# Attention products: another order of PSUM banks, row copies on GpSimd, casts behind bank copies, joint exponentials

## The chip, the cores and the metric

The kernel runs on one core of one Trainium2 chip. It is written in Python with a tile framework that places tiles, inserts semaphores and orders the instructions of each engine. The metric is the device time of one execution in microseconds (us); the median of several runs is compared. A profile of one execution shows each instruction's start and length on five engines: TensorE (PE; its weight loads are PEld), VectorE (DVE), ScalarE (ACT), GpSimd (POOL) and SyncE (SP, which here only issues DMAs).

## The reference: what is computed

One sequence of 512 tokens of width 1024 passes two layers, each a mixer and a SwiGLU feed-forward block. The change touches only the mixer of the first layer, dilated window attention:

```python
proj = (xn @ w_in).reshape(B, S, N_GROUPS, 3, ATTN_HEADS, ATTN_HEAD_DIM)
for g, (window, dilation) in enumerate(((128, 1), (512, 4), (2048, 16))):
    q = apply_partial_rope(proj[:, :, g, 0], positions) * scale
    k = apply_partial_rope(proj[:, :, g, 1], positions)
    o, lse = dilated_window_attention(q, k, proj[:, :, g, 2], window, dilation)
wts = jax.nn.softmax(jnp.stack(lses), axis=0)
o = jnp.einsum('gbsh,gbshd->bshd', wts, jnp.stack(outs))
```

There are 8 heads of 128 and three groups of queries, keys and values. Group 0 attends to a window of 128 neighbours; groups 1 and 2 see every 4th and every 16th token. Only the first 32 of a head's 128 dimensions are rotated by position (`apply_partial_rope`). The three groups' results are joined by a softmax over their log sums. After attention come the output projection and the feed-forward block; the second layer has an mLSTM mixer and another feed-forward block. All matrices are fp32.

## The kernel before

**Products in three parts.** A fp32 matrix is split into a high part, rounded to a shorter format (a cast on ScalarE, L223), and a low part, the rest (a subtraction on VectorE, L225). A product is the sum of high x high, high x low and low x high (`SPLITS`).

**Head pairs.** Heads are worked on in four pairs (`pr` 0 to 3). For each pair `project_pair` makes queries and keys of the three groups. Group 0 is a plain product (`project`, two chunks of weights for q and two for k, 128x512 matmuls). Groups 1 and 2 of pairs 1 to 3 go through `qk_unit`: a Strassen-like scheme of seven half-size products with 24 matmuls of 128x256 each, in the order P1, P5, P6, P2, P7, P3, P4. Their sums live in three PSUM banks: `c11` (P1, P2), `p5` (P5, P3) and `u` (P6, P7, P4). `u` starts as a copy of P1's result, made by ScalarE (L905), and P6 adds to it. After each product `finish` empties or combines a bank: P5 and P6 are copied to `vu` (L908, L910), P2 and P4 go to the query tile by two ScalarE copies (L899 takes the 32 rows to be rotated, L918 all 128), and P7 and P3 are added to `vu` on VectorE (L925). The tag `acc` has three banks in all; who asks for a bank gets one that has come free and waits for its last reader.

**Weights.** `feed` holds a plan of weight preparations. `prepare_part` subtracts weight blocks on VectorE where a product needs it (L873), splits the block (L223, L225) and issues the next loads on SP (L865). `feed.pop` takes the next prepared weights, `feed.fill(n)` prepares until `n` are ready, three to four products ahead.

**Rotation.** `rope` rotates the packed 32 rows on VectorE (L607 to L616) and returns `back`, which copies the rotated rows back into the query and key tiles. For the plain products (`blocks` true) these are eight copies of 32x256 on ScalarE (L622); they are put off by three ticks in pairs 1 to 3.

**Attention of the pair before.** While pair `pr` is projected, attention of pair `pr - 1` runs between its products. A counter of ticks orders this: `advance` adds one and runs what is due. Group 0 of a pair has four ticks; in `qk_unit` a tick falls after P5, P2, P3 and P4. `RUN_AT` gives the ticks, counted from the pair's start: scores of groups 1 and 2 at 1 (`scores12`), the five steps of `rest` at 4, 5, 8, 8, 9, values at 11 and 12, loads of values at 2, 3, 1. Scores of group 0 (`scores0`) of the pair now projected come at its tick 10.

Scores are masked on VectorE (L706, L727), which also takes row maxima; `exponentials` runs on ScalarE: for group 0 four per head (L743), for groups 1 and 2 eight per head (L749) of 128x128, whose sums are added on VectorE (L751). `joint` computes the weights of the groups, `weigh` multiplies them in (L794, L797), `transposes` turns the probabilities in blocks of 32 (L803) and writes them to DRAM by four DMAs (L806), `bring` reads them back transposed (L811), and `values` multiplies them with the values (L821, L826) into a bank of tag `o`, which `scores0` uses too.

**What sets the order.** The framework puts instructions on each engine's queue in the order in which the kernel traces them, unless an earlier one is not ready by its own plan; then a later one may go ahead. Explicit edges restrict this: `issue_after(ins)` puts what is traced inside it behind `ins` on the same engine. `behind_scores` puts weight subtractions behind the last masking of group 0's scores (`ahead_of_splits`), `behind_factors` puts weight casts behind the ScalarE instruction kept in `ahead_of_casts`, and `behind(fn, engine=ACT)` puts a function's ScalarE work behind the last that was traced. Each engine then runs its queue strictly in order. DMAs of the attention steps are issued by POOL, loads of weights by SP.

Of the kernel before, what the change touches and what calls it, by code (L numbers as in the profile page):

```python
# [36 lines left out]
RUN_AT = (1, (4, 5, 8, 8, 9), (11, 12), (2, 3, 1))  # L37
# [36 lines left out]
def tile_hybrid_dilated_attn_mlstm(  # L74
# [329 lines left out]
    with ExitStack() as actx:  # L404
# [198 lines left out]
        def rope(qk, rot, blocks, first=0, end=4, direct=False):  # L603

            at = slice(R * first, R * end)
            a, sh = rot[0][at], rot[1][at]
            nc.vector.stream_shuffle(sh, a, shift)  # L607
            nc.vector.tensor_tensor(a, a, cosn[at], op=ALU.mult)
            nc.vector.tensor_tensor(sh, sh, sinn[at], op=ALU.mult)
            two_m = lambda t: t.rearrange("p (m s) -> p m s", m=2)  # L610
            if direct:
                for q in range(first, end):
                    nc.vector.tensor_tensor(halves(qk[q // 2][:R], q % 2), two_m(rot[0][quarter(q)]),
                                            two_m(rot[1][quarter(q)]), op=ALU.add)
                return
            nc.vector.tensor_tensor(a, a, sh, op=ALU.add)  # L616

            def back():
                for q in range(first, end):
                    if blocks:  # L620
                        for m in range(2):
                            nc.scalar.activation(turned(qk, q, m, True), packed(rot, q, m, True), AF.Copy)  # L622
                    else:
                        nc.scalar.activation(halves(qk[q // 2][:R], q % 2), two_m(rot[0][quarter(q)]), AF.Copy)
            return back
# [28 lines left out]
        def attention_pair(pr, qks):  # L654
# [3 lines left out]
            dn = ap2.tile([P, 2, 2, 4], F32, tag="dn", name=nm + "dn", bufs=2)  # L658
# [32 lines left out]
            def scores0(q, k):  # L691
# [19 lines left out]
                for i in range(2):  # L711
                    exponentials(0, i)
# [21 lines left out]
            def exponentials(o, i):  # L734
# [11 lines left out]
                for g in (1, 2):  # L746
                    for c in range(4):
                        blk = p12[i][:, 4 * (g - 1) + c, :]
                        nc.scalar.activation(blk, blk, AF.Exp, bias=nb[:, 1, i, c:c + 1], scale=QK_SCALE,  # L749
                                             accum_out=dn[:, g - 1, i, c:c + 1])  # L750
                nc.vector.tensor_tensor(own[:, 1, 1, i], dn[:, 0, i], dn[:, 1, i], op=ALU.add)  # L751
# [85 lines left out]
            rest = (first_rest, lambda: transposes(0), lambda: weigh(1), lambda: (transposes(1), bring(0)),  # L837
# [52 lines left out]
        def qk_unit(pr, g, qk):  # L890
# [10 lines left out]
            def finish(name):  # L901
                nonlocal rot, vu
                if name == "P1":
                    acc["u"] = acc_tile(nm + "u")
                    nc.scalar.activation(acc["u"], acc["c11"], AF.Copy)  # L905
                elif name == "P5":
                    vu = ap.tile([P, 2, SEQ], F32, tag="vu", name=nm + "vu")
                    nc.scalar.activation(vu[:, 0], acc["p5"], AF.Copy)  # L908
                elif name == "P6":
                    nc.scalar.activation(vu[:, 1], acc["u"], AF.Copy)  # L910
                elif name in ("P2", "P4"):
# [6 lines left out]
                    nc.scalar.activation(halves(qk[0], th), src, AF.Copy)  # L918
                    if last and th:
                        rope(qk, rot, False, 1, 2, True)  # L920
                else:
# [9 lines left out]
            for n, name in enumerate(QK_ORDER):  # L931
                key = target[name]
                if name in ("P1", "P5"):
                    acc[key] = acc_tile(nm + key)
                whl = feed.pop()
# [12 lines left out]
                feed.fill(feed.ahead + 1)  # L948
# [6 lines left out]
                if n in (1, 3, 5, 6):  # L955
                    advance()

        def project_pair(pr, qks, then=None):
            nm = "a%d" % pr
            for g in range(3):  # L960
# [18 lines left out]
                for part in range(2):  # L979
# [24 lines left out]
                    if part == 1:  # L1004
# [3 lines left out]
                        else:  # L1008
                            back = turn()
                            defer(3 if pr else 1, lambda back=back: behind(back, engine=ACT))  # L1010
# [1360 lines left out]
```

## Time and profile before

| what | us |
|---|---|
| median of 3 runs | 1405.29 |
| lowest and highest of them | 1402.56, 1406.05 |
| profiled execution, its own time | 1400.59 |
| its span, first to last instruction | 1398.8 |

The profile names a group of instructions by line, engine, operation, the tile written and the tiles read, and its shape. "Busy" is time in which the engine works; a wait is idle time before an instruction, put down to what released it. In a timeline row the numbers are the start and the length; in square brackets stand the idle time before it and its releaser. A row of windows gives for a stretch its length, then for each engine the busy time and the number of instructions, then the share of full speed that TensorE's clock was granted, the busy share of the DMA engines and GB/s. In names, `a1g2p` is bank `p5` of pair 1, group 2, `P_h` and `P_l` are the high and low parts of product weights, `W` a weight block, `a0pB` and `a0pT` the turned and the fetched probabilities of pair 0, `a1s` scores and `a1o` values of pair 1. Tile names drop numbers, so `P_h` stands for every product.

### The profile page before, as it was taken

To read this page: it belongs to the slowest core of one execution; us is meant where nothing else is said; L and a number is where in the kernel's file an instruction comes from. 1 tells how busy PE (TensorE), PEld (TensorE's weight loads), DVE (VectorE), ACT (ScalarE), POOL (GpSimd) and SP (SyncE) were. 2 spreads that over 40 slices of the span, in tenths; PEclk is the share of its full clock that TensorE was granted. 3 is DMA by queue.
4 is the path that set the end of the run, shared out by engine and by line. 5 is a ranking of instruction groups with operands and counts; after the bars stand their busy time and mean duration, and the time that the engine had idled before them with its cause. 6 is when DMAs were issued, how large, how long until landed. Compare 5 with 4: busy or idle time off the path is not lost. (4 is left out here: it accounts for less than half of the span.)

```text
span 1398.8 us, 22646 instructions
## 1 busy us (share of the span) xinstructions
PE 1374.3 (98%) x8740; PEld 1247.2 (89%) x8740; DVE 1110.6 (79%) x1853; ACT 799.1 (57%) x1334; POOL 163.8 (12%) x240
## 2 busy tenths in 40 slices
PE   9999999999999999999999999999999999999997
PEld 7888889989988888999999998898888899999886
DVE  7758768595878289877877898898858987888887
ACT  5556565756665155445566464786534544458854
POOL 3000011111001001000000100113201240001213
PEclk9999999999999999999999999999999999999999
DMA  8534246538274447333253643324334563335963
GB/s 288 181 120 136 83 144 194 161 95 258 76 266 141 159 130 158 121 121 115 91 164 84 159 129 93 91 76 106 99 113 117 139 189 121 121 107 132 199 164 101
DMA packets 140068, 193.82 MB, mean 139 GB/s; under 512 B 8980, under 2 KB 104788, under 8 KB 139960
## 3 DMA queue, kind: packets, MB, share of 16 engines
q1 hardware_dynamic: 119552, 139.81, 31.3%
q0 software_dynamic: 18752, 51.43, 15.6%
q8 instruction: 69, 1.13, 0.3%
q10 hardware_dynamic: 1656, 1.12, 0.2%
q14 instruction: 39, 0.32, 0.1%
HBM read 167.30 MB, written 22.54 MB: 136 GB/s over the span
## 5 line engine op out<-in xcount | busy, mean ns | idle before, releaser
L1674 POOL DMA_DIRECT2D f1T<-in_ffn_w_out_dram x15 | 17.8, 1186 | 209.1 <-DMA f1P_2w_w<-in_ffn_w_out_dram 136.6
L1649 POOL DMA_DIRECT2D f0S<-in_ffn_w_out_dram x10 | 8.8, 886 | 259.6 <-DVE f0hid L1566 173.1
L2206 POOL DMA_DIRECT2D hD<-hB x32 | 21.8, 698 | 68.5 <-DVE hB L2203 68.5
L255 PE MATMUL mo<-n_h,mo_k_l 128*128 128x512 f32 x64 | 25.3, 395 | 0.0
L255 PE MATMUL mo<-n_h,mo_k_h 128*128 128x512 f32 x64 | 25.2, 394 | 0.0
L255 PE MATMUL mo<-n_l,mo_k_h 128*128 128x512 f32 x64 | 25.2, 393 | 0.0
L255 PE MATMUL awo<-ao_h,awo_k_h 128*128 128x512 f32 x64 | 25.2, 393 | 0.0
L255 PE MATMUL mqk<-n_h,mqk_k_h 128*128 128x512 f32 x64 | 25.1, 392 | 0.0
L255 PE MATMUL mwo<-yo_l,mwo_k_h 128*128 128x512 f32 x64 | 25.1, 392 | 0.0
L255 PE MATMUL mqk<-n_l,mqk_k_h 128*128 128x512 f32 x64 | 25.1, 392 | 0.0
L255 PE MATMUL awo<-ao_l,awo_k_h 128*128 128x512 f32 x64 | 25.0, 391 | 0.0
L255 PE MATMUL f0j<-n_h,f0j_h 128*128 128x512 f32 x64 | 25.0, 391 | 0.0
L255 PE MATMUL f1j<-n_h,f1j_h 128*128 128x512 f32 x64 | 25.0, 391 | 0.0
L255 PE MATMUL mwo<-yo_h,mwo_k_l 128*128 128x512 f32 x64 | 25.0, 391 | 0.0
L255 PE MATMUL mqk<-n_h,mqk_k_l 128*128 128x512 f32 x64 | 25.0, 390 | 0.0
L255 PE MATMUL awo<-ao_h,awo_k_l 128*128 128x512 f32 x64 | 25.0, 390 | 0.0
L255 PE MATMUL f0j<-n_h,f0j_l 128*128 128x512 f32 x64 | 24.9, 390 | 0.0
L255 PE MATMUL f1j<-n_h,f1j_l 128*128 128x512 f32 x64 | 24.9, 390 | 0.0
L255 PE MATMUL f0j<-n_l,f0j_h 128*128 128x512 f32 x64 | 24.9, 389 | 0.0
L255 PE MATMUL f1j<-n_l,f1j_h 128*128 128x512 f32 x64 | 24.9, 389 | 0.0
L255 PE MATMUL mwo<-yo_h,mwo_k_h 128*128 128x512 f32 x64 | 24.8, 391 | 0.0
L225 DVE TENSOR_TENSOR v1P_l<-v1W,v1P_h 128x1024 fp32r<-128x1024 f32 x14 | 17.1, 1224 | 9.3 <-ACT v1P_h L223 9.3
(2617 smaller groups left out, 5899.7 us busy)
## 6 DMA issues: line engine op xcount, KB each, us to landing
f0j_w<-in_ffn_w_in_dram SPq DMA_DIRECT2D x17, 512.0 KB, 5.2
f1j_w<-in_ffn_w_in_dram SPq DMA_DIRECT2D x17, 512.0 KB, 6.1
f1T<-in_ffn_w_out_dram POOLq DMA_DIRECT2D x15, 512.0 KB, 7.0
f0hid<-in_ffn_w_in_dram SPq DMA_DIRECT2D x9, 512.0 KB, 5.7
f1hid<-in_ffn_w_in_dram SPq DMA_DIRECT2D x9, 512.0 KB, 4.9
v0W<-in_attn_w_in_dram SPq DMA_DIRECT2D x8, 512.0 KB, 6.4
v1W<-in_attn_w_in_dram SPq DMA_DIRECT2D x8, 512.0 KB, 3.7
awo_k_w<-in_attn_w_out_dram SPq DMA_DIRECT2D x8, 512.0 KB, 6.3
```

Of the source, the lines that this page charges most:

```text
L225: nc.vector.tensor_tensor(lo[:, :n], raw[:, :n], hi[:, :n].bitcast(F32), op=ALU.subtract)
L255: nc.tensor.matmul(acc, whl[a][:, k, m * P:(m + 1) * P], pairs[b][kk], start=(kk == 0 and (a, b) == SPLITS[0]), stop=(kk == nk - 1 and (a, ...
L1649: nc.gpsimd.dma_start(t, src[1][:, ks], accum_op=ALU.add)
L1674: nc.gpsimd.dma_start(view(to), weight_rows(hk * UNITS + u, n), accum_op=ALU.add)
L2206: nc.gpsimd.dma_start(hD[k // 4].rearrange("(b i) x -> i b x", i=R)[:, :, c0:c0 + R], t[R * a_:R * (a_ + 1)])
```

## The change

Seven edits, all in the attention mixer:

1. In `qk_unit`, bank `u` is asked for, and filled from `c11`, ahead of P5's matmuls and after P5's own bank, no longer right after P1.
2. The copies of rotated rows of the plain products (pairs 1 to 3) move from ScalarE, three ticks late, to GpSimd, one tick late.
3. After each bank copy `ahead_of_casts` is set to it, so later weight casts stand behind it on ScalarE.
4. `feed.fill` comes after `advance` instead of ahead of it, not after P1, and once more ahead of P5.
5. Exponentials of groups 1 and 2 share one instruction of 128x256 per block; the tile `dn` and the additions at L751 go.
6. In the last pair, group 0's exponentials are put off by two ticks and stand behind ScalarE's other work.
7. The first head's transposed probabilities are fetched (`bring(0)`) at tick 7 as a step of its own; it was done at tick 8 after the second transpose.

```diff
--- before.py
+++ after.py
@@ -34,7 +34,7 @@
 C2 = float(np.float32(np.uint32(np.float32(TWO_PI - C1).view(np.uint32) & 0xFFFFF000).view(np.float32)))
 C3 = float(np.float32(TWO_PI - C1 - C2))
 SCORES0_AT = 6
-RUN_AT = (1, (4, 5, 8, 8, 9), (11, 12), (2, 3, 1))
+RUN_AT = (1, (4, 5, 7, 8, 8, 9), (11, 12), (2, 3, 1))
 LAST_AT = (1, (2,), (), (1, 1, 1))
 STACK_AT = (9, 11, 15, 17)
 HEAD_AT = ((9, 10, 12), (10, 11, 13), (12, 13, 15), (13, 14, 16), (15, 16, 18), (16, 17, 19), (18, 19, 21),
@@ -615,11 +615,15 @@
                 return
             nc.vector.tensor_tensor(a, a, sh, op=ALU.add)
 
-            def back():
+            def back(by_pool=False):
                 for q in range(first, end):
                     if blocks:
                         for m in range(2):
-                            nc.scalar.activation(turned(qk, q, m, True), packed(rot, q, m, True), AF.Copy)
+                            to, src = turned(qk, q, m, True), packed(rot, q, m, True)
+                            if by_pool:
+                                nc.gpsimd.tensor_copy(to, src)
+                            else:
+                                nc.scalar.activation(to, src, AF.Copy)
                     else:
                         nc.scalar.activation(halves(qk[q // 2][:R], q % 2), two_m(rot[0][quarter(q)]), AF.Copy)
             return back
@@ -655,7 +659,6 @@
             nm = "a%d" % pr
             mx = ap2.tile([P, 2, 2, 4], F32, tag="mx", name=nm + "mx", bufs=2)
             nb = ap2.tile([P, 2, 2, 4], F32, tag="nb", name=nm + "nb", bufs=2)
-            dn = ap2.tile([P, 2, 2, 4], F32, tag="dn", name=nm + "dn", bufs=2)
             own = ap2.tile([P, 2, 2, 2, 4], F32, tag="own", name=nm + "own", bufs=2)
             oth = ap2.tile([P, 2, 2, 2, 4], F32, tag="oth", name=nm + "oth", bufs=2)
             p, p0, p12 = [], [], []
@@ -708,8 +711,14 @@
                                 sp[:, o:o + w], mask_band[:, 2 * P - w:], 1.0, -3e38,
                                 op0=ALU.add, op1=ALU.max, accum_out=own[:, 0, 0, i, b:b + 1])
                 ahead_of_splits[0] = last_on(DVE)
-                for i in range(2):
-                    exponentials(0, i)
+
+                def exps():
+                    for i in range(2):
+                        exponentials(0, i)
+                if pr < HEADS // 2 - 1:
+                    exps()
+                else:
+                    defer(2, lambda: behind(exps, engine=ACT))
 
             banks_ = {}
 
@@ -743,12 +752,10 @@
                         nc.scalar.activation(blk, blk, AF.Exp, bias=nb[:, 0, i, b:b + 1], scale=QK_SCALE,
                                              accum_out=own[:, 1, 0, i, b:b + 1])
                     return
-                for g in (1, 2):
-                    for c in range(4):
-                        blk = p12[i][:, 4 * (g - 1) + c, :]
-                        nc.scalar.activation(blk, blk, AF.Exp, bias=nb[:, 1, i, c:c + 1], scale=QK_SCALE,
-                                             accum_out=dn[:, g - 1, i, c:c + 1])
-                nc.vector.tensor_tensor(own[:, 1, 1, i], dn[:, 0, i], dn[:, 1, i], op=ALU.add)
+                for c in range(4):
+                    blk = p12[i].rearrange("p (g c) k -> p c g k", g=2)[:, c]
+                    nc.scalar.activation(blk, blk, AF.Exp, bias=nb[:, 1, i, c:c + 1], scale=QK_SCALE,
+                                         accum_out=own[:, 1, 1, i, c:c + 1])
 
             def exchange():
 
@@ -834,7 +841,7 @@
             def first_rest():
                 joint()
                 weigh(0)
-            rest = (first_rest, lambda: transposes(0), lambda: weigh(1), lambda: (transposes(1), bring(0)),
+            rest = (first_rest, lambda: transposes(0), lambda: bring(0), lambda: weigh(1), lambda: transposes(1),
                     lambda: bring(1))
             if pr == HEADS // 2 - 1:
                 def all_rest():
@@ -900,14 +907,13 @@
 
             def finish(name):
                 nonlocal rot, vu
-                if name == "P1":
-                    acc["u"] = acc_tile(nm + "u")
-                    nc.scalar.activation(acc["u"], acc["c11"], AF.Copy)
-                elif name == "P5":
+                if name == "P5":
                     vu = ap.tile([P, 2, SEQ], F32, tag="vu", name=nm + "vu")
                     nc.scalar.activation(vu[:, 0], acc["p5"], AF.Copy)
+                    ahead_of_casts[0] = last_on(ACT)
                 elif name == "P6":
                     nc.scalar.activation(vu[:, 1], acc["u"], AF.Copy)
+                    ahead_of_casts[0] = last_on(ACT)
                 elif name in ("P2", "P4"):
                     th = int(name == "P4")
                     src = two_m(acc[target[name]])
@@ -916,9 +922,10 @@
                         rot = t[:, 0], t[:, 1]
                     pack(th, src[:R])
                     nc.scalar.activation(halves(qk[0], th), src, AF.Copy)
+                    ahead_of_casts[0] = last_on(ACT)
                     if last and th:
                         rope(qk, rot, False, 1, 2, True)
-                else:
+                elif name in ("P7", "P3"):
                     th = int(name == "P7")
                     out = halves(qk[1], th)
                     with behind_scores():
@@ -932,6 +939,11 @@
                 key = target[name]
                 if name in ("P1", "P5"):
                     acc[key] = acc_tile(nm + key)
+                if name == "P5":
+                    acc["u"] = acc_tile(nm + "u")
+                    nc.scalar.activation(acc["u"], acc["c11"], AF.Copy)
+                    ahead_of_casts[0] = last_on(ACT)
+                    feed.fill(feed.ahead + 1)
                 whl = feed.pop()
                 with fenced():
                     for m in range(2):
@@ -945,7 +957,6 @@
                                                  start=(name in ("P1", "P5") and m == 0 and k == 0 and (a, b) == SPLITS[0]),
                                                  stop=(m == 1 and k == 3 and (a, b) == SPLITS[-1]), skip_group_check=True)
                 finish(name)
-                feed.fill(feed.ahead + 1)
                 if n == 6 and not last:
                     back = rope(qk, rot, False)
                     if g == 2:
@@ -954,6 +965,8 @@
                         defer(1, lambda: behind(back, engine=ACT))
                 if n in (1, 3, 5, 6):
                     advance()
+                if n:
+                    feed.fill(feed.ahead + 1)
 
         def project_pair(pr, qks, then=None):
             nm = "a%d" % pr
@@ -1007,7 +1020,7 @@
                             postponed.append(lambda: turn()())
                         else:
                             back = turn()
-                            defer(3 if pr else 1, lambda back=back: behind(back, engine=ACT))
+                            defer(1, (lambda back=back: back(True)) if pr else lambda back=back: behind(back, engine=ACT))
                     if pr == 0 and 1 <= g:
                         step = 2 * (g - 1) + part
                         (lambda: sum_of("S3"), lambda: sum_of("S4"), lambda: None, lambda: None)[step]()
```

## The prediction

> **What bounds the kernel now.** I read the page first, then the waits of the attention stage, then windows and timelines around each wait.
>
> ```profile
> span 1398.8 us, 22646 instructions
> PE 1374.3 (98%) x8740; PEld 1247.2 (89%) x8740; DVE 1110.6 (79%) x1853; ACT 799.1 (57%) x1334; POOL 163.8 (12%) x240
> ```
>
> TensorE is busy for 1374.3 of 1398.8 us. The edit removes no matmul, so it can win only idle time of TensorE, or matmuls that run slowly. The edited code runs from 178 to 480 us; there TensorE waits for this (us in total, times, longest):
>
> ```profile
> PE a2g2p L944 <- ACT a2g_q L918: 2.8, 1, 2.8
> PE a3g2p L944 <- ACT a3g_q L918: 2.8, 1, 2.8
> PE a1g2p L944 <- ACT a1g_q L918: 2.8, 1, 2.8
> PE a3o L821 <- DMA a3pT<-a3pD: 1.1, 1, 1.1
> PE a3s L724 <- DVE a3g_q L613: 1.0, 1, 1.0
> PE a1o L821 <- DVE a2own L706: 0.7, 1, 0.7
> ```
>
> Three waits are one event, once in each of the head pairs 1 to 3: product P5 of group 2 waits for the copy at L918 that empties the last product of group 1. The next fence has one stretch of two undisturbed products (P5 and P6 of pair 1, group 1), then the stretches from the start of P1 to the start of P6 in group 2 of the three pairs. Its columns are length, busy time by engine, granted clock, DMA share and GB/s.
>
> ```profile
> 208.62:214.36 5.74, 5.74 (x50) 5.74 (x49) 5.74 (x19) 3.10 (x4) 0.00 (x0) 1.00 0.31 94
> 226.17:236.44 10.27, 7.50 (x51) 7.30 (x50) 10.16 (x15) 7.61 (x15) 2.73 (x5) 0.83 0.37 93
> 306.48:315.29 8.81, 6.01 (x50) 5.81 (x49) 8.56 (x13) 7.64 (x15) 2.55 (x5) 1.00 0.16 35
> 386.30:396.61 10.31, 7.52 (x50) 7.31 (x49) 10.07 (x14) 7.64 (x15) 2.73 (x5) 0.83 0.27 64
> ```
>
> Two products take 5.74 us; here they take 10.27, 8.81 and 10.31, an excess of 4.53, 3.07 and 4.57, together 12.2 us. Some 8.4 of it is the wait itself. The rest is the clock: in pairs 1 and 3 it falls to 0.83 over the stretch and busy time grows by 1.5 us against pair 2, whose equally long wait left it at 1.00.
>
> The Trainium skill ("TensorE: Matmul & The Clock Gate", What's actually happening) says the clock halves after an idle window of about 3.4 us, on a free-running window. By 3.4 us alone no wait of 2.8 us should cost clock, and 3 us of the excess would stay; the trace has two that did, and it decides.
>
> Why does P5 wait? On ScalarE, with the first matmul of P5 last:
>
> ```profile
> 227.77 1.45 ACT L622 ACTIVATE a1g_q<-rot 32x256 f32<-32x256 f32 x4
> 229.23 1.45 ACT L622 ACTIVATE a1g_k<-rot 32x256 f32<-32x256 f32 x4
> 230.71 0.59 ACT L899 ACTIVATE rot<-a1g1u 32x512 f32<-32x512 f32 x1
> 231.32 0.60 ACT L918 ACTIVATE a1g_q<-a1g1u 128x512 f32<-128x512 f32 x1
> 231.94 1.06 ACT L223 ACTIVATE a1g2P_h<-a1g2W 128x1024 fp32r<-128x1024 f32 x1
> 232.91 0.58 ACT L905 ACTIVATE a1g2u<-a1g2c 128x512 f32<-128x512 f32 x1
> 231.97 0.39 PE L944 MATMUL a1g2p<-S,a1g2P_h 128*128 128x256 f32 x1 [2.77 <-ACT a1g_q L918]
> ```
>
> P5 starts 0.05 us after L918 ends. So the bank that P5 writes is the one P4 of group 1 filled (`u`): `u` of group 2 was asked for first and took the bank that came free first, P3's. And L899 and L918 stand behind eight plain-row copies (L622), 2.91 us.
>
> **The change part by part.**
>
> Banks in another order. P5 now asks for its bank before `u` does, so it gets P3's, emptied by VectorE long before; only the copy into `u` needs P4's, and its reader P6 starts one product (2.87 us) later. ScalarE then has L899, L918 and the copy to do after P4, 0.59 + 0.60 + 0.58 = 1.8 us. Moving L622 away is a second cure: L899 could start at 227.77, and L918 would end near 229.0, when P5 is due (226.17 + 2.87 = 229.04). I take the whole 12.2 us as removed; what is late next is VectorE, below. If only the wait went and the clock still fell, 9 would be gained; a loss is excluded, since no instruction is added to this chain.
>
> Plain rows on GpSimd. Eight copies of 32x256 per pair leave ScalarE for POOL, two ticks earlier, right after the rotation's add ends (214.5 in pair 1). Their readers are the first scores, which TensorE reaches after P2 of group 2, at 226.17 + 4 x 2.87 = 237.7, some 23 us later, so their own length is hidden. Behind them in POOL's queue stand the four issues of the first transpose, which wait until 218.98 for L803; a delay of some us there is covered, because the values that read this data come five ticks later. The price to fear is VectorE:
>
> ```profile
> 198.00:240.00 42.00, 39.19 (x282) 37.45 (x281) 41.17 (x64) 26.56 (x44) 5.47 (x10) 0.96 0.41 120
> 214.53 2.36 DVE L225 TENSOR_TENSOR a1g1P_l<-a1g1W,a1g1P_h 128x1024 fp32r<-128x1024 f32 x2
> 216.80 2.18 DVE L803 STREAM_TRANSPOSE a0pB<-a0p 128x1920 f32<-128x1920 f32 x1
> 222.46 0.69 DVE L925 TENSOR_TENSOR a1g_k<-a1g1u,a1g1vu 128x512 f32<-128x512 f32 x1
> 223.20 0.38 PE L944 MATMUL a1g1u<-xa_h,a1g1P_h 128*128 128x256 f32 x1
> 233.08 1.22 DVE L225 TENSOR_TENSOR a1g2P_l<-a1g2W,a1g2P_h 128x1024 fp32r<-128x1024 f32 x1
> L452 POOL COPY sinn<-angles 32x128 f32<-32x128 f32 x4 | 1.2, 291 | 0.1
> L2067 POOL CAST ql<-ql 64x512 fp32r<-64x512 f32 x8 | 8.4, 1052 | 82.7 <-DVE ql L2066 59.6 <-DVE m0rr L2120 18.3 <-DVE m1rq_a L193 4.7
> L2066 DVE TENSOR_TENSOR ql<-mqk,qs x8: 673/685/1007, 885.0 to 943.5; 64x512 fp32r<-64x512 f32 x8
> 898.15 1.13 POOL L2067 CAST ql<-ql 64x512 fp32r<-64x512 f32 x1 [10.63 <-DVE ql L2066]
> 898.82 1.01 DVE L2066 TENSOR_TENSOR ql<-mqk,qs 64x512 fp32r<-64x512 f32 x1
> ```
>
> VectorE (third number of the window) is busy for 41.17 of these 42 us. L925 at 222.46 ends just as P4 starts, so lateness there goes straight to TensorE; the low part of P2's weights (ends 234.3) will be wanted at 229.04 + 2 x 2.87 = 234.8. And the two engines disturb each other: a cast on POOL runs from 898.15 to 899.28, and the subtraction beside it takes 1.01 us where 0.685 is usual, 0.32 more.
>
> The Trainium skill ("SBUF — State Buffer", SBUF: two separate sides) states it as an exclusive lock: a two-input VectorE operation and a GpSimd one that reads SBUF never overlap, and the loser is blocked for the whole instruction. The trace agrees in this pair of rows. By that rule each of the eight copies costs VectorE its full length unless it falls beside an operation with one input.
>
> No row has a 32x256 copy on POOL. Below: nothing, if all fall beside L803, which reads one tensor. Above: 1.05 us each (L2067). A copy of 32x128 takes 0.29; with twice the elements I take 0.4. Some five fit beside L803 (2.18 us); three meet subtractions at 0.27 (somewhat under the 0.32 of a larger cast): 0.8 us per pair, on the path through L925. Three pairs: 2.4 us lost.
>
> Casts behind bank copies; fills after the tick's work. Now each weight cast (1.06) stands behind the bank copy of its product instead of ahead. The bank copy waits for TensorE; behind it on ScalarE wait the cast and what follows, behind the cast VectorE's subtraction. Casts run three products ahead, so 1 us later costs nothing while ScalarE has room (3.10 busy of 5.74); without that room TensorE would wait the excess. The fills also issue the next weight loads on SP, now behind the tick's work; each waits there for the split that frees its buffer, and nothing else is in that queue between two fills of a pair, so I book zero. The order matters at the first scores:
>
> ```profile
> 246.72 1.06 ACT L223 ACTIVATE a2g0q_k_h<-a2g0q_k_w 128x1024 fp32r<-128x1024 f32 x1 [4.60 <-DMA a2g0q_k_w<-in_attn_w_in_dram]
> 247.81 1.23 DVE L225 TENSOR_TENSOR a2g0q_k_l<-a2g0q_k_w,a2g0q_k_h 128x1024 fp32r<-128x1024 f32 x1 [4.43 <-ACT a2g0q_k_h L223]
> 248.95 0.28 DVE L706 CUSTOM_DVE_ANT_0 a1p<-a1s,acst 128x128 f32<-128x128 f32 x1
> ```
>
> The split of the next pair's weights, late by its DMA, stands ahead of the masking of scores (L706), whose banks the values need: the 0.7 us wait of `a1o`. Tracing the scores before the fill puts L706 first. I book 0.7 us, though this order must come out, or TensorE, four us earlier, waits there far longer (rival two).
>
> Exponentials of two groups at once. Sixteen of 128x128 become eight of 128x256 per pair, and two additions of 0.16 us (L751) go:
>
> ```profile
> L749 ACT ACTIVATE a1p<-a1p,a1nb 128x128 f32<-128x128 f32 x16 | 6.2, 394 | 3.6 <-DVE a1nb L738 3.6
> L743 ACT ACTIVATE a1p<-a1p,a1nb 128x256 f32<-128x256 f32 x6 | 3.0, 498 | 0.0
> 197.05 0.16 DVE L751 TENSOR_TENSOR a0own<-a0dn 128x4 f32<-128x4 f32 x1 [1.56 <-ACT a0p L749]
> ```
>
> 16 x 0.394 - 8 x 0.498 = 2.3 us of ScalarE per pair, while TensorE waits for nothing: zero on the path. The group-1 casts start earlier, and VectorE, idle for 1.56 us at this place, gets a head start; I do not book it.
>
> Last pair: group 0's exponentials run two ticks later, behind ScalarE's other work.
>
> ```profile
> 417.62 1.28 ACT L899 ACTIVATE rot<-a3g_k 32x512 f32<-32x512 f32 x2
> 418.94 0.01 DVE L607 LOAD_MASK_SELECT rot<-rot  x1 [3.33 <-ACT rot L899]
> L749 ACT ACTIVATE a3p<-a3p,a3nb 128x128 f32<-128x128 f32 x16 | 6.2, 394 | 7.8 <-DVE a3nb L738 7.8
> ```
>
> They held up L899 and with it the rotation that `a3s` waits for. I book that wait of 1.0 us; the displaced exponentials, some 4 us (the six large of such a set take 3.0), fit into ScalarE's 7.8 us of idle before L749.
>
> First transpose fetched at once. One DMA issue moves ahead of the second transpose's four on POOL. Its data (8.9 us from issue to landing, median of the two `pT` loads) is not waited for in pairs 0 to 2, so this is worth zero; it waits at the head of POOL's queue for the first four to land, and would cost something only if that held back the second four, which come with the second transpose, three ticks behind the first.
>
> ```profile
> DMA to landing us min/median/max: 8.6/8.9/9.1
> ```
>
> Sum: -12.2 - 0.7 - 1.0 + 2.4 = -11.5 us. The profiled execution took 1400.59 us (span 1398.8 and 1.8 around it), so this gives 1389.1. The median of the runs, 1405.29, lies 4.7 us above the profiled execution; the forecast for a median is 1405.3 - 11.5 = 1393.8.
>
> **The rivals.**
>
> One: VectorE cannot follow. All eight copies block it at 0.4 us: 3.2 per pair, 9.6 in all, leaving 13.9 - 9.6 = 4.3: 1401.0. For it speaks the full VectorE; against it L803, and the head start from the shorter exponentials.
>
> Two: the wait only moves. If L706 stays behind the late split, whose DMA sets its time, its end does not move, and the values now come due just with it (the 0.7 us in pair 2, nothing in pair 1). The 4 us won in each pair are then returned, and about 1 of 13.9 remains: 1404. For it speak the idle times of 4.60 and 4.43 us above; against it the order in which the scores are now traced.
>
> Three, slower: POOL's copies are dear. At L2067's 1.05 us each, blocking VectorE throughout, 8 x 3 x 1.05 = 25.2 against 13.9: 1416.6. It decides above 0.58 us of blocking per copy (13.9 / 24). For it speaks that those casts did take 1.05 beside VectorE; against it that much of that span was waiting for VectorE.
>
> Four: the bank is not exchanged. Then the second cure leaves P5 waiting some 0.1 us, and the time is that of the forecast; I give it no chance of its own.
>
> **How the numbers follow.** Forecast 0.70, with a range of its own of 1389 to 1399; rival one 0.12, two 0.06, three 0.12. A measurement here tells 0.3% (4.2 us) from no change. The forecast and somewhat over half of rival one are faster (0.77), the rest of it and rival two the same (0.11), rival three slower (0.12). The range runs from 1388.5 (all 13.9 us, the last wait for `a3pT`, and 2 us of scatter) to 1402, which takes in rival one and leaves out two and three.
>
> **What would show it.** The three L944 waits for L918 are gone, and the clock reads 1.00 in the P1-to-P6 stretches, each near 5.74 us. POOL shows eight copies per pair near 0.4 us between 214 and 223; VectorE subtractions beside them stretch to 1.4 or so, and P4 of group 1 waits under 1 us for L925. L706 follows the first scores without the late split ahead. `a3s` waits for nothing. The prediction is wrong if TensorE has new waits above 1 us per pair at L925, at the low parts (L225), or at `a0o` to `a2o`.

## The result, and the profile after

The changed kernel takes 1394.08 us (median of 4 runs, 1393.86 to 1396.64) against 1405.49 us: a ratio of 0.9927, 95% interval 0.9909 to 0.9945. Run again beside the kernel before it gave 0.9935 (0.9920 to 0.9949). The forecast was 1393.8 us. The size was right; several steps that led to it were not.

The page of the profiled execution after (1396.64 us, the longest of the four), its span and its busy times:

```profile
span 1394.9 us, 22560 instructions
PE 1371.6 (98%) x8740; PEld 1245.1 (89%) x8740; DVE 1111.5 (80%) x1845; ACT 779.8 (56%) x1246; POOL 178.7 (13%) x264
```

What TensorE waits for in the attention stage (178 to 480 us) of that execution, in the columns of the prediction's list (L956 is L944 of before, L733 is L724, L1001 is L988, L906 is L899):

```profile
PE a3s L733 <- DVE a3g_q L613: 2.6, 1, 2.6
PE a2g1p L956 <- DVE a2g_k L1001: 2.0, 1, 2.0
PE a3g1p L956 <- DVE a3g_k L1001: 2.0, 1, 2.0
PE a1s L733 <- ACT a1g_k L628: 1.5, 1, 1.5
PE a2s L733 <- ACT a2g_k L628: 1.5, 1, 1.5
```

The three waits of P5 in group 2 are gone, and so are those of `a1o` and `a3o`. The windows from P1 to P6 of group 2, which were 10.27, 8.81 and 10.31 us long:

```profile
225.48:231.24 5.76, 5.76 (x50) 5.76 (x49) 5.76 (x11) 3.68 (x5) 0.56 (x1) 1.00 0.45 156
305.35:311.06 5.71, 5.71 (x51) 5.71 (x50) 5.68 (x9) 5.22 (x7) 0.56 (x1) 1.00 0.49 171
387.10:392.86 5.76, 5.76 (x50) 5.76 (x49) 5.39 (x9) 5.51 (x8) 0.36 (x1) 1.00 0.50 171
```

Two products take 5.7 to 5.8 us here at full clock, so the three stretches win 12.2 us against the first profile of before, as forecast. But the spans of the two profiled executions, 1398.8 and 1394.9, differ by 3.9 us only. The new waits account for that: -12.2 (windows) - 0.7 (`a1o`) - 1.1 (`a3o`) + 1.6 (`a3s`, 1.0 to 2.6) + 4.0 (two waits for L1001) + 3.0 (two for L628) + 1.5 (a fall of the clock, below) = -3.9. So the medians, 11.4 us apart, hold something that the first profile of before does not show. That was the first question.

**Where the new waits come from.** VectorE in pair 2, before and then after. L988/L1001 is the second copy of group 0's `k` out of its bank, which P5 of group 1 is to fill:

```profile
286.21 0.17 DVE L780 TENSOR_TENSOR a1ee<-a1oth,a1cf 128x16 f32<-128x16 f32 x1
286.55 0.69 DVE L988 COPY a2g_k<-a2g0k 128x512 f32<-128x512 f32 x1 [0.17 <-PE a2g0k L255]
```

```profile
285.21 1.07 DVE L801 TENSOR_SCALAR a1p<-a1p,a1cf 128x128 f32<-128x128 f32 x4
286.20 1.13 DVE L804 TENSOR_SCALAR a1p<-a1p,a1cf 128x256 f32<-128x256 f32 x4
287.25 0.68 DVE L1001 COPY a2g_k<-a2g0k 128x512 f32<-128x512 f32 x1
```

Before, the copy stood in the middle of the chain of instructions that compute the factors of the weighing, straight behind its matmuls. After, the whole chain and the weighing of the first head's probabilities (L801, L804; 2.2 us) stand ahead of it, and P5 starts at 288.08 where it was due near 285.9.

The wait for L628 (group 2's rotated rows, which the scores `a1s` read) is set on ScalarE. After:

```profile
250.99 1.06 ACT L223 ACTIVATE a2g0k_k_h<-a2g0k_k_w 128x1024 fp32r<-128x1024 f32 x1 [2.76 <-DMA a2g0k_k_w<-in_attn_w_in_dram]
251.96 0.39 ACT L752 ACTIVATE a1p<-a1p,a1nb 128x128 f32<-128x128 f32 x1
...
257.73 0.59 ACT L906 ACTIVATE rot<-a1g2u 32x512 f32<-32x512 f32 x1
...
262.24 1.27 ACT L628 ACTIVATE a1g_q<-rot 32x512 f32<-32x512 f32 x2 [1.87 <-DVE rot L616]
```

P4 ends at 252.07; its pack (L906 at 257.73) stands behind the eight exponentials of group 0 (L752, to 255.8), and these behind a cast that waits for its weights. Before, the exponentials ran at the same time (251.6 to 255.5), but P4 ended at 257.4. TensorE now comes 5 us earlier and the exponentials do not: the row maxima that they need are ready at 248.0, but the late cast is ahead of them in ScalarE's queue. Before, that cast (of the same tile, at 256.81) stood behind them.

### The profile page after: what moved, and what is told of

The parts are those of the page before. It is cut to its first block, busy times and chain, and to the rows that moved or that the text cites. A ratio compares the mean times of both kernels' runs of the same rounds, so it can differ in the third digit from the quotient of the medians.

```text
span 1394.9 us, 22560 instructions
## 1 busy us (share of the span) xinstructions
PE 1371.6 (98%) x8740; PEld 1245.1 (89%) x8740; DVE 1111.5 (80%) x1845; ACT 779.8 (56%) x1246; POOL 178.7 (13%) x264
```

## The experiments

**Both kernels again.** No edit; more runs and a second profile of each.

> The kernel before, unchanged, for a second profile beside five rounds of times. Open: the medians of before and after lie 11.4 us apart, but the two profiled executions only 3.9 (1400.59 against 1396.64). Theory A: the profiled execution of before was a lucky one. Then this profile stands near its own runs at 1405, some 4 to 5 us longer than the first profile, and the time shows either as a third fall of the clock (pair 2, group 2, 1.5 us) or as later transfers outside the attention stage. Theory B: the profile of before is always about 4 us quicker than its runs without profile, and then 11.4 us is not what the trace of before can show. Ratio 1.000 within 0.002 in both.

> The changed kernel, unchanged, on the same chip as the kernel before. Ratio 0.990 to 0.994. The profiled execution after was 2.6 us longer than its other runs. Theory A: that was the fall of the clock at P5 of group 1 in pair 3 (0.86, some 1.6 us), which depends on chance; this profile then shows either no fall there or a span near 1392.5. Theory B: the profile of this kernel is always longer, by the profile's own load on the DMA queues; then the wait of a3s for the late casts of a3g12v (2.6 us) is again there at full length.

Measured: before 1404.14 (1401.09 to 1405.85) beside 29 more runs of it at 1404.47 (1400.35 to 1407.47); after 1394.61 (1393.04 to 1396.46), ratio 0.9935 (0.9920 to 0.9949). The waits of the attention stage in the second profile of before, span 1403.6, and then of after, span 1393.1 (those above 0.3 us):

```profile
PE a2o L821 <- DVE a3own L706: 4.8, 1, 4.8
PE a2g2p L944 <- ACT a2g_q L918: 2.8, 1, 2.8
PE a3g2p L944 <- ACT a3g_q L918: 2.8, 1, 2.8
PE a1g2p L944 <- ACT a1g_q L918: 2.7, 1, 2.7
PE a1o L821 <- DVE a2own L706: 2.1, 1, 2.1
PE a3o L821 <- DMA a3pT<-a3pD: 1.6, 1, 1.6
```

```profile
PE a3g1p L956 <- DVE a3g_k L1001: 2.0, 1, 2.0
PE a1s L733 <- ACT a1g_k L628: 1.6, 1, 1.6
PE a3s L733 <- DVE a3g_q L613: 1.2, 1, 1.2
PE a2s L733 <- ACT a2g_k L628: 0.5, 1, 0.5
PE a2g1p L956 <- DVE a2g_k L1001: 0.4, 1, 0.4
```

Theory A holds, but not with its reason: what the first profile of before lacked is not a third fall of the clock but the wait for L706. It cost 0.7 us there and 6.9 here. The masking of the first scores stands behind a split whose cast waited for its weights; here VectorE was idle for 6 us before it:

```profile
409.91 1.23 DVE L225 TENSOR_TENSOR a3g12v_k_l<-a3g12v_k_w,a3g12v_k_h 128x1024 fp32r<-128x1024 f32 x1 [6.02 <-ACT a3g12v_k_h L223]
413.79 0.27 DVE L706 CUSTOM_DVE_ANT_0 a3p<-a3s,acst 128x128 f32<-128x128 f32 x1
```

The changed kernel has no such wait in either profile. On the second profiles the gain is 10.5 us, near the medians'. The stretches from P1 to P6 are 10.25, 8.79 and 8.79 us in the second profile of before and 5.76, 5.70 and 5.76 in that of after: 10.6 us, not 12.2, because the clock fell behind one of the three waits and not behind two.

**The bank alone, the rows alone.** The first edit of the change by itself, then the second by itself.

```diff
 banks_only
-                if name == "P1":
-                    acc["u"] = acc_tile(nm + "u")
-                    nc.scalar.activation(acc["u"], acc["c11"], AF.Copy)
...
                     acc[key] = acc_tile(nm + key)
+                if name == "P5":
+                    acc["u"] = acc_tile(nm + "u")
+                    nc.scalar.activation(acc["u"], acc["c11"], AF.Copy)
 rows_only
...
-                            defer(3 if pr else 1, lambda back=back: behind(back, engine=ACT))
+                            defer(1, (lambda back=back: back(True)) if pr else lambda back=back: behind(back, engine=ACT))
```

> Kernel before with the exchanged bank alone: P5 takes its bank ahead of u, and the copy into u is traced just ahead of P5. Rows stay on ScalarE. My theory (two cures, each nearly sufficient, the bank being one): P5 no longer waits; P6 then waits for the copy into u, which on ScalarE stands behind eight row copies, L899, L918 and a cast: it ends near 233.5 in pair 1 where P6 is due at 231.9, so P6 waits 0.6 (copy ahead of the cast) to 1.6 us in each pair instead of 2.8, and the clock is won back (3.0 us). In exchange P5 of group 1 in pairs 2 and 3 now gets the bank of group 0's last product and waits for its evacuation, 1 to 2 us each. Sum: -3.6 to -6.6 for the waits, -3.0 for the clock, +2 to +4: ratio 0.994 to 0.999. Rival: the new wait at group 1 and its clock take everything back: ratio 0.999 to 1.003.

> Kernel before with the plain rows alone on GpSimd, one tick behind the rotation. My theory: P5 of group 2 then waits at most 0.1 us for L918 in the three pairs and the clock stays at 1.00 (-12 us), no bank is exchanged, so P5 of group 1 has no new wait; VectorE loses up to 2.4 us to the copies. Ratio 0.991 to 0.993, as good as the whole change. Rival one: the masking of the first scores still stands behind the late split (L225), so TensorE, four us earlier, waits for it at the values of pairs 0 to 2, and three quarters come back: ratio 0.997 to 0.999. Rival two: the copies block VectorE and TensorE waits at L925 or at a low part: 0.998 or more.

Measured: the bank alone 1402.44, ratio 0.9995 (0.9982 to 1.0008); the rows alone 1403.73, ratio 1.000 (0.999 to 1.001). The waits of the bank alone, then of the rows alone:

```profile
PE a3g2p L946 <- ACT a3g_q L917: 2.8, 1, 2.8
```

```profile
PE a0o L825 <- DVE a1own L710: 5.2, 1, 5.2
PE a2o L825 <- DVE a3own L710: 2.0, 1, 2.0
```

Neither time is the one that my theory gave. The first edit does nothing that these runs can tell: P5 still waits in all three pairs (2.8, 2.8 and 2.7 us) for the copy that empties P4's bank. The built programs say why. The framework's planner gives out the three banks of `acc`, and the products get the same ones whichever asks first:

```
bank of        a1g1 c11 p5 u   a1g2 c11 p5 u
before              5   3  4        5   4  3
after               5   3  4        5   4  3
```

It is so in pairs 2 and 3 too: the banks are the same before and after. The rows are the cure of the waits for L918 (0.2 us is left in each of pairs 2 and 3), and they alone win nothing: TensorE comes to the values of the pair before earlier and waits there for the masking (L710 here, L706 before). This is rival two of the prediction, in a kernel that lacks the order of the fills.

**The fills alone, rows and fills.** In both kernels the next cast is traced behind the tick's work; the second has the rows of `rows_only` as well.

```diff
                 finish(name)
-                feed.fill(feed.ahead + 1)
...
                     advance()
+                feed.fill(feed.ahead + 1)
```

> Kernel before with one edit: in the units of groups 1 and 2 the next cast is traced behind the tick's work, not ahead of it. Rows, banks, exponentials, fetches as before. Theory: the masking of the first scores (L706) then stands ahead of the late split of the next pair's weights, so the waits of a1o and a2o for L706 are gone (0.7 us in the first profile of before, 2.1 + 4.8 in the second); they are also what makes the times of before scatter over 7 us. The three waits of P5 for L918 (2.8 each) and their clock stay. So about 1399.5: ratio 0.995 to 0.998, with a scatter of 3 us or less. Rival: the scatter has another source and the values wait for something else by then: ratio 0.999 to 1.001.

> Kernel before with two edits: plain rows on GpSimd one tick behind the rotation, and the next cast behind the tick's work. No other bank order, no merged exponentials, no early fetch. Theory: each cures what the other leaves: no wait for L918 and none for L706. The second copy out of the bank of group 0's k stands ahead of the weighing in VectorE's queue here (it does not in the changed kernel), so P5 of group 1 does not wait either. 1404.5 - 12 (waits and clock) - 5 (L706, its mean) + up to 3 (group 2's scores of pairs 0 to 2 come sooner than their rows): 1388 to 1391.5, ratio 0.988 to 0.991, better than the whole change. Rival: the other edits are needed for the gain: ratio 0.994 or more.

Measured: fills alone 1400.91 (1398.44 to 1406.18), ratio 0.9978 (0.9964 to 0.9993); rows and fills 1398.98, ratio 0.9955 (0.9939 to 0.9971). The waits with the fills alone, then with both:

```profile
PE a2g2p L944 <- ACT a2g_q L918: 2.6, 1, 2.6
...
PE a3s L724 <- DVE a3g_q L613: 2.1, 1, 2.1
```

```profile
PE a3s L728 <- DVE a3g_q L613: 3.4, 1, 3.4
PE a2g1u L948 <- DVE a2g_k L929: 1.7, 1, 1.7
PE a3g1u L948 <- DVE a3g_k L929: 1.6, 1, 1.6
PE a3s L728 <- ACT o_keep L640: 1.5, 1, 1.5
```

The order of the fills takes the waits for L706 away and is worth 3.1 us by itself (0.22%); that it would narrow the scatter to 3 us was wrong. With the rows it is worth 6.3, more than 3.1 and 0, though the two intervals overlap a little: each edit cures what the other runs into. What I expected of the two (0.988 to 0.991) missed by half, because two other things came up: VectorE cannot follow at L929 (3.8 us over the pairs with 0.5 in pair 1; rival one, at a smaller price), and the last scores wait 4.9 us.

**What else the change holds.** From the changed kernel: the exponentials apart again, and the casts not tied to the bank copies.

```diff
 unmerged
-                for c in range(4):
-                    blk = p12[i].rearrange("p (g c) k -> p c g k", g=2)[:, c]
+                for g in (1, 2):
+                    for c in range(4):
+                        blk = p12[i][:, 4 * (g - 1) + c, :]
...
+                nc.vector.tensor_tensor(own[:, 1, 1, i], dn[:, 0, i], dn[:, 1, i], op=ALU.add)
 no_cast_order (at four places)
-                    ahead_of_casts[0] = last_on(ACT)
```

> Changed kernel with the exponentials of groups 1 and 2 apart again (sixteen of 128x128 and two additions per pair), all else as after. Theory: the merge is what put the second copy out of the bank of group 0's k behind the weighing (a place in VectorE's queue, not time on ScalarE); with the exponentials apart it stands ahead again, and the waits of a2g1p and a3g1p for L1001 (2.0 + 2.0, or 0.4 + 2.0, with a fall of the clock in pair 3 of some 1.6) go. 1390.5 to 1392.5, ratio 0.990 to 0.9915. Rival: ScalarE's 2.3 us per pair are needed, since TensorE now waits for ScalarE's L628 at the scores: a1s and a2s wait longer and the ratio is 0.9935 or more.

> Changed kernel without the four notes that put each weight cast of the units behind the bank copy of its product; the next cast is still traced behind the tick's work. I booked this edit at zero. Kernel before with rows and fills alone stood at 1399 and waited at P4 of group 1 for the sum L932 (1.7 and 1.6 us in pairs 2 and 3, 0.5 in pair 1) and longer for the last scores (3.4 + 1.5); the changed kernel has neither. Theory: the order of the casts is the missing edit. Then these waits come back and the ratio is 0.995 to 0.997. Rival: the merged exponentials or the early fetch made the difference (the changed kernel with the exponentials apart had 0.9 us of that wait, in pair 3 alone): the ratio stays at 0.992 to 0.994.

Measured: exponentials apart 1394.50, ratio 0.9926 (0.9909 to 0.9943); no order of the casts 1395.18, ratio 0.9933 (0.9913 to 0.9952). Neither edit is worth anything that these runs can tell; I had expected 0.990 to 0.9915 of the first and 0.995 to 0.997 of the second. The mechanism I had for the first is there: with the exponentials apart the copy out of the bank stands at 285.71, ahead of the weighing at 291.26, and no wait for it is left.

```profile
285.71 0.69 DVE L1004 COPY a2g_k<-a2g0k 128x512 f32<-128x512 f32 x1
291.26 1.08 DVE L804 TENSOR_SCALAR a1p<-a1p,a1cf 128x128 f32<-128x128 f32 x4
```

Most of what it wins is spent elsewhere: against the second profile of after, 2.4 us of L1001 and 1.5 of clock are gone, and `a2s` has 1.0 more, `a3g1u` 0.9, `a3o` 0.6.

The order of the casts does change the picture. Without it there is no wait for L628 or at the last scores, but the values wait for the masking again:

```profile
PE a2o L828 <- DVE a3own L709: 3.2, 1, 3.2
```

A cast that waits for its weights (L223 at 399.73, 4.18 us idle before it) stands there ahead of the pack L906 on ScalarE, and so ahead of the rotation and the masking behind it on VectorE. So the fills alone do not always keep the masking early, and the edit exchanges one set of waits for another of the same size.

The gap between rows and fills (0.9955) and the whole change is thus neither of these two edits alone. The intervals of the two overlap, so the gap itself is not sharp. By the waits it may be the put-off exponentials of the last pair (4.9 us of waiting at the last scores against 1.2 to 2.6); that edit was not run alone, nor was the early fetch, so this is not shown.

**Place or engine, and the price of GpSimd.** From the changed kernel: the copies on ScalarE but at the early place, and the copies on GpSimd made twice.

```diff
 rows_act_early
-                            defer(1, (lambda back=back: back(True)) if pr else lambda back=back: behind(back, engine=ACT))
+                            defer(1, lambda back=back: behind(back, engine=ACT))
 rows_twice
                                 nc.gpsimd.tensor_copy(to, src)
+                                nc.gpsimd.tensor_copy(to, src)
```

> Changed kernel with the eight plain-row copies on ScalarE again, but at the changed kernel's early place (one tick behind the rotation, not three). It tells the engine from the place. Theory (place): what P5 of group 2 waited for was the two ticks by which the copies came late, so the early place alone cures it; ScalarE has some 2.6 us idle per product there, and VectorE no longer shares its time with GpSimd: ratio 0.9915 to 0.9935, as after or a little better. Rival (engine): 2.9 us of copies ahead of the copy L915 and the casts behind it are more than ScalarE can take, and TensorE waits at a low part or at L932 for over 1 us per pair: ratio 0.995 or more.

> Changed kernel in which GpSimd makes each of the eight plain-row copies per pair twice, the same data to the same place: 24 copies more. It measures the disputed price. My prediction's price (0.27 us of VectorE and of TensorE for each copy that meets a two-input operation, three in eight sheltered or not): the added ones lie later, beside subtractions and the weighing, so 24 x 0.27 = 6.5 us: ratio 0.9975. What the trace of after reads like: the copy pays (0.39 alone, 1.2 to 1.45 beside a subtraction), VectorE's subtraction is stretched by 0.2 at most and TensorE waits for none of it: ratio 0.9925 to 0.9945, unchanged. The exclusive lock at full length (1.05 each): 1.015.

Measured: on ScalarE early 1395.96, ratio 0.9938 (0.9921 to 0.9955), just above the range that I expected of the place; twice on GpSimd 1396.96, ratio 0.9952 (0.9934 to 0.9970). It was the place: with the copies two ticks earlier P5 of group 2 does not wait on ScalarE either, and the engine makes no difference that the intervals can tell. Twice the copies cost some 2.4 us against the changed kernel's 1394.6 (0.9935), between the two prices that I had expected: for 24 copies 0.1 us each. The intervals overlap, so it may be nothing; only their far ends, 7 us apart, would give 0.27 or more. The copies in the changed kernel, grouped (busy us, mean ns of one):

```profile
L624 POOL COPY a2g_q<-rot 32x256 f32<-32x256 f32 x4 | 1.5, 391 | 30.1 <-DVE rot L616 30.1
L624 POOL COPY a2g_k<-rot 32x256 f32<-32x256 f32 x4 | 3.4, 878 | 0.1
```

The first four run beside the transpose L810 (293.68 to 295.85), which reads one tensor, and take 0.39 us each, the prediction's estimate. The next four lie beside VectorE's subtractions, and there it is mostly GpSimd that loses: the mean more than doubles, while the longest of the seven subtractions for that product takes 1.42 us, against 1.23 before. Four weighings beside the last copy (L801 at 298.22, one tensor each) take 1.36 us, against 1.07.

**Against the new waits.** Two kernels made from the changed one. In both the weighing is traced a tick later; in one of them, `weigh_exps_later`, group 0's exponentials are also put off in pairs 1 and 2, as the change does in pair 3.

```diff
 both
-            rest = (first_rest, lambda: transposes(0),
+            rest = (joint, lambda: (weigh(0), transposes(0)),
 weigh_exps_later only
-                if pr < HEADS // 2 - 1:
+                if pr == 0:
                     exps()
```

> Changed kernel with two edits against its new waits. The weighing of the first head's probabilities is traced a tick later, with their transpose, so the copy out of the bank of group 0's k stands ahead of all but one of its parts: the waits for L1001 fall below 0.5 us each. Group 0's exponentials are put off by two ticks in pairs 1 and 2 as they are in pair 3, so the pack of P4 goes ahead of them and the rotated rows (L628) are there before group 2's scores: the waits of a1s and a2s go. Theory: 1394.4 - 2.4 to 5.6 - 2.1 to 3.0: 1386 to 1390, ratio 0.987 to 0.990, the fastest so far. Rival: the put-off exponentials hold up the casts behind them (a2g1P_h) or the exchange of the factors, and TensorE waits at a2g1c or a1xps: ratio 0.9925 or more.

> The faster version without its second edit: the weighing is traced a tick later, group 0's exponentials stand where the change put them. It tells which of the two new waits costs the time. Theory: the waits for L628 at group 2's scores do, with the clock that falls behind them (in the second profile of after and with the exponentials apart the stretch behind a1s's wait took 1.3 us longer). Then the waits for L1001 go (below 0.5 us) but most of the time stays, as it did with the exponentials apart: ratio 0.991 to 0.993. Rival: the waits for L1001 cost it (2.4 to 4.0 us and the clock at P5 of group 1): ratio 0.988 to 0.9895, near that of both edits.

Measured: with both edits 1386.73 (1386.35 to 1388.66), ratio 0.9874 (0.9855 to 0.9893), the fastest kernel here; the weighing alone 1390.89 (1389.05 to 1392.33), ratio 0.9912 (0.9897 to 0.9926). With both edits the copy out of the bank goes in behind one part of the weighing, and the rotated rows are ready at 260.4 for scores that start at 261.79:

```profile
282.33 0.29 DVE L801 TENSOR_SCALAR a1p<-a1p,a1cf 128x128 f32<-128x128 f32 x1
282.53 0.69 DVE L1001 COPY a2g_k<-a2g0k 128x512 f32<-128x512 f32 x1
```

```profile
253.15 0.59 ACT L906 ACTIVATE rot<-a1g2u 32x512 f32<-32x512 f32 x1
...
259.14 1.29 ACT L628 ACTIVATE a1g_k<-rot 32x512 f32<-32x512 f32 x2
```

The longest wait left in the attention stage is 0.5 us. The weighing alone gave the time that I expected, not the picture: its profile has no wait for L628, and the cast that waits for its weights starts 1 us sooner there (249.99); its longest wait is 1.8 us for probabilities that a DMA brings back (`a2pT`). So the wait for L628 was not shown to be the larger of the two. By the ratios the weighing is worth some 3 us and the exponentials some 5; each ratio's interval is 4 to 5 us wide, so neither size is sharp.

## Why the prediction was right, and which of its steps were not

- **P5's waits and their clock, -12.2 us: right, for half the reason.** The first profiles give 12.2, the second 10.6: whether the clock falls behind such a wait differs from one execution to the next, and the sum took over the two falls of one. "P5 now asks for its bank before `u` does, so it gets P3's" is wrong: it gets P4's as before (rival four, to which I gave no chance). What I called the second cure, the rows moved out of the way, is the whole cure, and by its early place, not by its engine. I read the rule for the banks off one case, where it fitted, and did not test it on the new order.
- **`a1o`, -0.7 us: mis-sized.** The step took one execution's wait for the size of a wait that a DMA sets. It is 0.7 in one profile and 6.9 in the other; the order of the fills alone is worth 3.1 us by the runs. The first profile of before, 4.7 us under the median, had met a short one.
- **`a3s`, -1.0 us: wrong.** It is 2.6 and 1.2 us after. Putting the exponentials off was booked as removing the wait, but TensorE arrives earlier, and the packs that the rotation needs (L906 at 414.75 in the first profile after) stand behind casts that wait for their weights (412.44, after 7.52 us of idle time). In the kernel with rows and fills, which lacks that edit among others, the last scores waited 4.9.
- **GpSimd's copies, +2.4 us: too dear.** In neither profile of the changed kernel does TensorE wait for VectorE's sums (L932). A copy beside the transpose costs 0.39 us as estimated; subtractions and weighings on VectorE are stretched by 0.2 to 0.3 us in a pair, GpSimd bears most of it, and 24 more copies cost 0.1 us each by the ratios, where 0.27 was booked. The Trainium skill ("SBUF — State Buffer", SBUF: two separate sides) says that whichever starts first holds the ports and the other blocks fully; the prediction charged VectorE whichever it was. The mean of 0.88 us for a blocked copy against 0.39 agrees for the loser; the small stretch on VectorE says that GpSimd was the loser for most of it.
- **The casts behind the bank copies and the merged exponentials, zero: right in the sum.** But the merge is not free of consequence: it moved the copy out of group 0's bank behind the weighing.
- **Not foreseen: 4.0 us at L1001, 3.0 at L628, and 1.5 of clock with them.** The text asked what is late next and named VectorE at L925, where nothing happened in the changed kernel. The waits came 40 to 65 us further on, around group 0 of the next pair. Both slacks could be read from the trace of before. The copy out of the bank ended at 287.24 and P5 began at 289.22, 2 us later; the merged exponentials let the chain and 2.2 us of weighing go ahead of that copy. The exponentials of group 0 were over at 255.5, 2 us ahead of P4's end, and TensorE was to come 4 us sooner. I followed neither the gain nor the new order that far.
- **The total: its size is partly luck.** On the profile from which the sum was made it failed: 1389.1 was forecast and the first profiled execution after took 1396.64. On the medians, what was missed on one side (7 us of new waits, their clock, `a3s`) was made up by what was too small or too dear on the other (L706 and `a3o`, GpSimd). That these cancel to 0.3 us is luck. The sign is not: -12.2 and the waits for L706 are real, and rivals one, two and three did not happen in the changed kernel. One and two did happen in kernels with only a part of it.

## What to carry to other kernels

A wait that a DMA sets has no size in one profile: look at the scatter of the runs, or profile twice, before it goes into a sum. When TensorE is sped up by a few microseconds, list the next places where it meets another engine, and how much slack each had, not only those beside the edit. A change of order in the source is not a change in the machine until the banks or queues of the built program say so; and two edits that win 0.2% and nothing alone can be worth more together (0.45% here), because each cures what the other runs into.

## What the runs showed of the hardware that was not expected

Waits of equal length do or do not cost clock. The stretch from a wait of P5 in group 1 to the next P2 in pairs 2 and 3 of the first profile after (waits of 2.05 and 1.99 us), in the columns of the windows above:

```profile
288.08:293.89 5.81, 5.81 (x48) 5.81 (x49) 5.81 (x9) 3.80 (x6) 0.00 (x0) 1.00 0.29 93
368.33:375.64 7.31, 7.31 (x48) 7.31 (x49) 7.31 (x9) 3.80 (x6) 1.45 (x4) 0.77 0.35 109
```

Two products took 5.81 us behind the first and 7.31 behind the second, 1.5 more. At `a1s` a wait of 1.52 us cost nothing in the first profile after (first row below). One of 1.65 in the second brought the clock to 0.81 (second row):

```profile
264.20:271.75 7.55, 7.54 (x41) 6.48 (x41) 5.83 (x37) 3.74 (x10) 0.00 (x0) 1.00 0.70 190
```

```profile
264.12:273.33 9.21, 9.21 (x40) 7.94 (x41) 7.50 (x41) 4.64 (x14) 0.00 (x0) 0.81 0.59 160
369.00:371.00 2.00, 2.00 (x12) 2.00 (x11) 2.00 (x3) 0.52 (x1) 0.00 (x0) 0.53 0.00 0
```

The last row lies behind the wait of `a3g1p` in that profile: the clock is near half speed for a while, and the low means of longer windows are this, diluted. The Trainium skill ("TensorE: Matmul & The Clock Gate", What's actually happening) puts the window at about 3.4 us and calls it free-running. The half speed and the chance in it agree with these rows; idle times of 1.65 to 2.0 us that set it off are shorter than that page leads one to expect. Of the waits between 1.5 and 3 us in the attention stage, in the two profiles of before and the two of after, 6 of 15 lowered the clock, and behind each of the six the mean over the next 8 us is 0.79, so they cost about the same. Over the profiles of all kernels here, none of the 25 waits from 0.6 to 1.59 us lowered it, 15 of the 31 from 1.65 to 2.80 did, and so did all four above 3. In a sum I would now book half of 1.5 us for each wait of 1.65 to 3 us, and nothing for a shorter one.
